# The sums of the input's quarters by accumulating transfers within SBUF, with the prompt's pieces spread over two stages

## The chip, the cores and the metric

The kernel runs on one core of one Trainium2 chip. The metric is the time of one execution on the device in microseconds (us), less being better. The five engines of the core appear under the profile's names: PE (TensorE matmuls; PEld is its loading of weights), DVE (VectorE), ACT (ScalarE), POOL (GpSimd) and SP (SyncE, which here only issues transfers).

## What is computed

One layer of a hybrid network is applied to 1024 tokens of a sample and to 128 tokens of a prompt, in f32, with a model width of 1024. Cut to what matters:

```python
h = rmsnorm(x, norm_g) * (1 + scale) + shift              # scale, shift, gate from silu(cond) @ w_ada + b_ada
u, v, g_a, c_q, c_kv, k_rope, g_b = split(h @ w_in)       # widths 512, 512, 512, 256, 128, 64, 512
a_out = gelu(u) * mix128(rmsnorm(gelu(v))) * silu(g_a)    # mixing of positions in chunks of 128
q = rmsnorm(c_q) @ w_uq;  k, val = split(rmsnorm(c_kv) @ w_ukv)   # 4 heads, rotary part of 64
attn = softmax(q @ k.T / sqrt(192)) @ val                 # the sample also reads 256 cached context tokens
y = x + gate * (concat(a_out, attn * silu(g_b)) @ w_o)
out = rmsnorm(y, final_g)                                 # new c_kv and k_rope of the prompt are outputs too
```

The sample and the prompt use the same weights; the prompt reads only itself.

## The kernel before

Every operand of a matmul is kept as two numbers, a rounded **high** value and the **low** remainder, and a product is made of three matmuls: high by high, high by low, low by high. Whatever is prepared for PE therefore takes two elementwise operations: a cast to the high value (on ACT at line 543, or on POOL at line 117) and a subtraction that leaves the low one (on DVE at line 114 for weights and sums; line 968 for the prompt's weights).

The stages, by the time of the profile: loading, normalising and the projection of `v` (to about 75 us); the projection of `c_q`, `c_kv` and `k_rope` ("the latents' projection", accumulators `zacc`), the rest of `v`, the mixing of positions and the gate's vector (`gps`) to 153.5 us; the **product phases** (153.5 to 320.4 us); folds, rotary parts and transposes (to 353 us); attention (to 560 us); the output projection (to the end).

In the product phases the sample's tokens are multiplied by the weights of `u`, `g_a` and `g_b`: 12 blocks of 128 channels, taken in six pairs j. The tokens are cut in two halves and the features in two halves, so the input is four quarters A11, A12, A21, A22 (tiles `area..`, each 128 x 4 x 2 x 512: four k, and high and low). The 2 x 2 block product is made with seven products instead of eight. They are called phases 1, 2, 5, 6, 7, 4 and 3, in this order for the pairs, the last two alternating. Each (phase, pair) is 12 matmuls `pr` at line 828. Four phases read sums of the quarters in place of a quarter: S1 = A21 + A22 (phase 5), S2 = S1 - A11 (phase 6), S3 = A22 - S2 (phase 7), S4 = A12 - S2 (phase 3). `sum_steps` makes them for each k with nine additions of 128 x 512 (a quarter is the sum of its high and its low half, so adding a quarter takes two), lines 937 to 951, into tiles `ss` and `sta`/`stb`; 36 in all. `own` then splits a sum into high and low and writes it over a quarter that is no longer needed (`area10` in phases 5 and 7, `area00` in 6 and 3).

The weights of a (phase, pair) are loaded by SP into `wr` tiles (`raw_load`), combined where the phase needs a combination (`tsum`), and split into `wop0..` (high) and `wop1..` (low).

The prompt's 128 tokens are multiplied by the same weights apart: `prompt_steps`, 24 **pieces** (six pairs j, four y). A piece is a load into `praw` by SP, a cast into `pw0..`, a low half into `pw1..`, and six matmuls into the accumulator `pps` at line 977.

The order of the instructions on each engine is made ahead of the run by the class `Plan`, a list scheduler. A step has a key, engines that may do it, a cost in us for each, the steps that it depends on, a priority, and resources that it takes and gives back (buffer places: `slot`, `raw`, `praw`, `pw`, `st`). Among the steps that are ready the one with the smallest priority number goes first. `VG` steps go to DVE if it is free and to POOL otherwise. `lag` is the time after a step's cost until its result counts as there. The resulting rows are executed in order on each engine, which wait for one another by semaphores. The prompt's matmuls have the priorities `PROMPTP` (per pair), its loads `PROMPTL`; the first load waits for `openB`, the end of the mixing and the latents' projection.

Of the kernel before, what the change touches and what calls it, by code (L numbers as in the profile page):

```python
# [18 lines left out]
P = 128  # L19
# [10 lines left out]
PROMPTP = (7.2, 7.8, 8.6, 9.2, 9.8, 10.4)  # L30
PROMPTL = (1.605, 1.625, 1.645, 1.665, 1.685, 1.705)
# [11 lines left out]
class Plan:  # L43
# [8 lines left out]
    def run(self):  # L52
        left = sorted(self.steps, key=lambda s: s[:2])
        back = []
        now = 0.0
        while left:
            for b in [b for b in back if b[0] <= now]:
                back.remove(b)
                self.resources[b[1]] += 1
            moved = False  # L60
            for s in left:
                _, _, key, engs, cost, fn, deps, takes, gives, lag = s
                free = [n for n, e in enumerate(engs) if self.free[e] <= now + 1e-6]
                if not free or any(self.made.get(d, 1e9) > now + 1e-6 for d in deps):
                    continue
                if any(self.resources[r] < takes.count(r) for r in takes):
                    continue
                for r in takes:
                    self.resources[r] -= 1
                eng = engs[free[0]]  # L70
                if len(engs) > 1:
                    cost = cost[free[0]]
                    fn(self.engines[eng])
                else:
                    fn()
                self.free[eng] = now + cost
                self.made[key] = now + cost + lag
                self.made[key + "!"] = now + cost
                back += [(now + cost + lag, r) for r in gives]
                left.remove(s)  # L80
                self.log.append((now, cost, eng, key))
                moved = True
                break
            if not moved:
                later = [t for t in (*self.free.values(), *self.made.values(), *(b[0] for b in back)) if t > now + 1e-6]
                assert later, [(s[2], [d for d in s[6] if d not in self.made], s[7]) for s in left]
                now = min(later)
# [9 lines left out]
def tile_hymba_step(ctx: ExitStack, tc: tile.TileContext, I, O):  # L97
# [441 lines left out]
    VG, COST = "VG", (0.75, 1.3)  # L539
# [215 lines left out]
    order = {"load": None, "high": None, "prompt": ["openB"], "ph": []}  # L755
# [16 lines left out]
    def weight_steps(ph, j, prio):  # L772
# [8 lines left out]
        if ph in (5, 6, 4):  # L781

            def total(e):
# [3 lines left out]
                else:  # L787
                    e.tensor_tensor(tsum[j], r(0), tsum[j], op=ALU.subtract)
# [6 lines left out]
        elif ph == 7:  # L795

            def total(e):
                e.tensor_tensor(r(0), r(0), r(1), op=ALU.subtract)
                leave(keys[1])
# [15 lines left out]
        step(f"w{ph}{j}", "V", 0.75, low, [f"wh{ph}{j}"], prio, gives=gives)  # L815
# [39 lines left out]
    def result_steps(ph, j):  # L855
# [27 lines left out]
        elif ph == 6:  # L883
            def fn():
                uu[j] = place(j, 1, 0) if gb else pools["b1"].tile([P, 512], F32, tag=f"u{j}", name=f"uu{j}")
                V.tensor_tensor(uu[j], s1[j], bk(), op=ALU.add)
# [3 lines left out]
        elif ph == 7:  # L890
            step(f"c7{j}", "V", 0.75, lambda: V.tensor_tensor(zz[j], zz[j], bk(), op=ALU.add), [m, f"uz{j}"], 1)
# [4 lines left out]
        elif ph == 4:  # L896
            step(f"c4{j}", "V", 0.75, lambda: V.tensor_tensor(s1[j], s1[j], bk(), op=ALU.add), [m, f"c22s{j}"], 1, gives=("psa",))
# [13 lines left out]
    def sum_steps():  # L911

        for k in range(4):
            cell = {}

            def own(x, ph, deps, k=k):
                step(f"ah{ph}.{k}", SG, HIGH, lambda e: rounded(e, MOVING[ph][:, k, 0, :], x()), deps, 2.2 + PHP[ph])

                def low():
                    lo_of(MOVING[ph][:, k, 1, :], x(), MOVING[ph][:, k, 0, :])  # L920
                    if ph == 7:
                        leave(("st", "b", k))

                step(f"a{ph}.{k}", "V", 0.75, low, [f"ah{ph}.{k}"], 2.2 + PHP[ph], gives=("st", "slot") if ph == 7 else ())

            def st(name, k=k, cell=cell):
                cell[name] = place_for(("st", name, k), f"st{name}{k}", [512])
                return cell[name]

            def s_new(k=k):  # L930
                ss[k] = pools["b2"].tile([P, 512], F32, tag=f"ss{k}", name=f"ss{k}")
                return ss[k]

            q = lambda a, i, k=k: f32(a[:, k, i, :])

            def s1z(e, k=k, cell=cell):
                e.tensor_tensor(ss[k], ss[k], cell["a"], op=ALU.add)
                leave(("st", "a", k))

            step(f"s1x.{k}", VG, COST, lambda e, q=q, st=st: e.tensor_tensor(st("a"), q(A21, 0), q(A21, 1), op=ALU.add), ["openB"], 3.0 + 0.01 * k, takes=("st", "slot"))  # L940
            step(f"s1y.{k}", VG, COST, lambda e, q=q, s_new=s_new: e.tensor_tensor(s_new(), q(A22, 0), q(A22, 1), op=ALU.add), ["openB"], 3.0 + 0.01 * k)
            step(f"s1z.{k}", VG, COST, s1z, [f"s1x.{k}", f"s1y.{k}"], 2.9, gives=("st", "slot"))
            own(lambda k=k: ss[k], 5, [f"s1z.{k}"])
            step(f"s2x.{k}", VG, COST, lambda e, k=k, q=q: e.tensor_tensor(ss[k], ss[k], q(A11, 0), op=ALU.subtract), [f"a5.{k}"], 3.2 + 0.01 * k)
            step(f"s2y.{k}", VG, COST, lambda e, k=k, q=q: e.tensor_tensor(ss[k], ss[k], q(A11, 1), op=ALU.subtract), [f"s2x.{k}"], 3.1)
            own(lambda k=k: ss[k], 6, [f"s2y.{k}", f"m1{NJ - 1}.{k}"])
            step(f"s3x.{k}", VG, COST, lambda e, q=q, st=st: e.tensor_tensor(st("b"), q(A22, 0), q(A22, 1), op=ALU.add), [f"s2y.{k}"], 3.4 + 0.01 * k, takes=("st", "slot"))
            step(f"s3y.{k}", VG, COST, lambda e, k=k, cell=cell: e.tensor_tensor(cell["b"], cell["b"], ss[k], op=ALU.subtract), [f"s3x.{k}"], 3.3)
            own(lambda cell=cell: cell["b"], 7, [f"s3y.{k}", f"m5{NJ - 1}.{k}"])
            step(f"s4x.{k}", VG, COST, lambda e, k=k, q=q: e.tensor_tensor(ss[k], q(A12, 0), ss[k], op=ALU.subtract), [f"a6.{k}", f"s3y.{k}"], 3.6 + 0.01 * k)  # L950
            step(f"s4y.{k}", VG, COST, lambda e, k=k, q=q: e.tensor_tensor(ss[k], ss[k], q(A12, 1), op=ALU.add), [f"s4x.{k}"], 3.5)
            own(lambda k=k: ss[k], 3, [f"s4y.{k}", f"m6{NJ - 1}.{k}"])
# [5 lines left out]
    def prompt_steps(n, j, prio):  # L958
# [21 lines left out]
        for y in range(4):  # L980
# [4 lines left out]
            step(f"pw{j}{y}", VG, COST, lambda e, y=y: low(e, y), [f"ph{j}{y}"], 1.5, gives=("praw", "slot"))  # L985
# [23 lines left out]
        step(f"pa{j}", "S", 0.45, act, [f"pm{j}3", *deps], 1.5, takes=("slot",), gives=("pst",))  # L1009
        step(f"pt{j}", "T", 0.22, tr, [f"pa{j}"], 3, takes=("pst",), gives=("slot",))  # L1010
# [339 lines left out]
    with tc.manual_schedule(engines=engines):  # L1350
        plan.resources.update(psa=1, pst=2, slot=6, gv=3, ga=1, raw=4, wop=3, tmp=2, praw=2, pw=2, st=3, r2=1)
# [38 lines left out]
        for h in range(4):  # L1390
            qn_steps(0, 512, h, 19.5 + 0.1 * h, [f"s4y.{k}" for k in range(4)])
# [584 lines left out]
```

## Time and profile before

| | |
|---|---|
| median of 3 runs | 663.19 us (lowest 660.75) |
| profiled execution | 662.15 us, its span on the core 660.4 us |
| granted TensorE clock, mean | 0.973 |
| PE busy | 618.8 us, 94% |
| DVE busy | 437.3 us, 66% |
| ACT busy | 301.6 us, 46% |
| POOL busy | 225.4 us, 34% |
| moved by transfers | 60.48 MB, 92 GB/s over the span |
| chain that ended last | PE 75%, DVE 11%, issue 4%, DMA 4%, ACT 2%, POOL 2% |

The span is the time from the first to the last instruction on the core; the execution takes 1.75 us more. Busy time counts neither register and branch instructions nor the issuing of transfers. A stretch A:B is in us from the span's start. In a group's row, "128x512" is partitions by elements, "xN" the number of instructions, then busy time in us and the mean of one in ns, then the engine's idle time before them and what ended it.

### The profile page before, as it was taken

Reading aid. Unit: us, or ns where it says so; the run is one execution under the profiler, and the core shown is the slowest. Engines: PE = TensorE matmul, PEld = TensorE weight load, DVE = VectorE, ACT = ScalarE, POOL = GpSimd, SP = SyncE. Lnnn points to the kernel's source line nnn. Section 1 sums busy time; section 2 is a strip of 40 time slices with the busy share of each in tenths; the row PEclk is TensorE's granted clock in tenths of the full one; section 3 lists DMA queues with packets and bytes.
Section 4 is the critical chain, followed back from the end, with each engine's and each line's share of the span. In section 5 each row is a group of like instructions: output and inputs, shape, how many; then the busy total and the mean of one; then the engine's idle time right before and its main releaser. Section 6 shows DMA issues by size and latency. Waiting matters only on the chain.

```text
span 660.4 us, 9804 instructions
## 1 busy us (share of the span) xinstructions
PE 618.8 (94%) x3567; PEld 524.7 (79%) x3567; DVE 437.3 (66%) x874; ACT 301.6 (46%) x672; POOL 225.4 (34%) x203
## 2 busy tenths in 40 slices
PE   7799999999888899799988999999999999999995
PEld 6477887788667678578867799999999998888884
DVE  4334645525999978988476765667767766296755
ACT  4355873324333253355564655555555462132222
POOL 3523311106876667644452322223313332000001
PEclk9699999999878999999997999999999999999998
DMA  8971314302425562430010000000000012523221
GB/s 325 341 260 47 134 46 166 126 33 68 139 78 187 171 213 80 140 128 1 26 48 1 1 1 0 1 1 1 1 33 33 33 65 97 191 97 128 80 80 64
DMA packets 29840, 60.48 MB, mean 92 GB/s; under 512 B 3024, under 2 KB 13664, under 8 KB 29792
## 3 DMA queue, kind: packets, MB, share of 16 engines
q1 hardware_dynamic: 29648, 59.67, 26.6%
q8 instruction: 28, 0.46, 0.3%
q14 instruction: 20, 0.16, 0.1%
q10 hardware_dynamic: 144, 0.20, 0.1%
HBM read 55.03 MB, written 4.83 MB: 91 GB/s over the span
## 4 chain that ended last, share of the span: by engine, by line
PE 75%; DVE 11%; issue 4%; DMA 4%; ACT 2%; POOL 2%; SPq 0%; ACTq 0%; POOLq 0%; DVEq 0%
PE pr L828 11%; PE pT L1504 5%; PE w L1754 5%; PE w L1753 5%; PE w L1755 5%; PE s L1461 3%; PE o L1528 3%; PE o L1530 3%; PE s L1465 3%; PE s L1462 3%; PE s L1463 3%; PE o L1529 3%; PE s L1464 3%; PE vacc L390 3%; PE pps L977 2%
## 5 line engine op out<-in xcount | busy, mean ns | idle before, releaser
L828 PE MATMUL pr<-area,wop 128*128 128x512 f32 x504 | 128.4, 403 | 4.3 <-ACT wop L543 2.3
L828 PEld LDWEIGHTS pr<-area,wop 128*128 128x128 f32 x504 | 93.8, 193 | 25.5 <-ACT wop L543 3.6
L1452 POOL TENSOR_SCALAR e<-e,rs 128x1280 f32<-128x1280 f32 x32 | 43.0, 1344 | 141.2 <-DVE rs L1451 126.3
L114 DVE TENSOR_TENSOR pl<-pT,ph 128x512 fp32r<-128x512 f32 x81 | 55.4, 687 | 45.9 <-ACT ph L1508 45.7
L1446 ACT ACTIVATE e<-s,nb,scl 128x256 f32<-128x256 f32 x64 | 56.1, 881 | 39.3 <-DVE nb L1440 39.2
L1508 ACT CAST ph<-pT 128x512 fp32r<-128x512 f32 x80 | 45.5, 590 | 40.0 <-PE pT L1504 37.2
L1753 PE MATMUL w<-area,areap 128*128 128x512 f32 (+1 forms) x152 | 57.8, 381 | 0.0
L1755 PE MATMUL w<-area,ml 128*128 128x512 f32 (+1 forms) x152 | 57.5, 378 | 0.0
L1754 PE MATMUL w<-area,areap 128*128 128x512 f32 (+1 forms) x152 | 57.5, 378 | 0.0
L1504 PE MATMUL pT<-ident,e 128*128 128x128 f32 x320 | 47.9, 272 | 0.6 <-DVE pl L114 0.6
L1528 PE MATMUL o<-ph,vh 128*128 128x256 f32 x160 | 48.0, 300 | 0.0
L1530 PE MATMUL o<-ph,vl 128*128 128x256 f32 x160 | 45.0, 281 | 0.0
L1529 PE MATMUL o<-pl,vh 128*128 128x256 f32 x160 | 44.9, 280 | 0.0
L1504 PEld LDWEIGHTS pT<-ident,e 128*128 128x128 f32 x320 | 37.8, 140 | 4.3 <-DVE pl L114 1.5
L1436 DVE TENSOR_REDUCE m<-s 128x1 f32<-128x1024 f32 x32 | 38.9, 1216 | 2.5 <-PE s L1465 2.5
L1461 PE MATMUL s<-kch,area 128*128 128x512 f32 (+1 forms) x96 | 38.8, 404 | 0.8 <-DVE areap L114 0.8
L977 PE MATMUL pps<-pw,areap 128*128 128x256 f32 x144 | 25.9, 312 | 13.1 <-DVE pw L968 13.1
L977 PEld LDWEIGHTS pps<-pw,areap 128*128 128x128 f32 x144 | 23.6, 210 | 17.1 <-DVE pw L968 14.5
L1844 POOL TENSOR_TENSOR z<-y,fg 128x256 f32<-128x256 f32 (+1 forms) x3 | 3.0, 998 | 95.4 <-DVE y L1839 95.4
L1463 PE MATMUL s<-kch,area 128*128 128x512 f32 (+1 forms) x96 | 34.7, 361 | 0.0
L1462 PE MATMUL s<-kcl,area 128*128 128x512 f32 (+1 forms) x96 | 34.7, 361 | 0.0
L1465 PE MATMUL s<-krl,area 128*128 128x512 f32 (+1 forms) x96 | 34.7, 361 | 0.0
(377 smaller groups left out, 1560.4 us busy)
## 6 DMA issues: line engine op xcount, KB each, us to landing
wr<-in_w_t SPq DMA_DIRECT2D x54, 256.0 KB, 3.4
ada<-in_ada_ss SPq DMA_DIRECT2D x16, 512.0 KB, 6.7
praw<-in_w_t SPq DMA_DIRECT2D x24, 256.0 KB, 3.3
xr<-in_x SPq DMA_DIRECT2D x9, 512.0 KB, 3.8
adag<-in_ada_g SPq DMA_DIRECT2D x8, 512.0 KB, 3.7
wor<-in_w_o SPq DMA_DIRECT2D x8, 512.0 KB, 3.7
out_y<-y SPq DMA_DIRECT2D x8, 512.0 KB, 2.8
x<-in_x SPq DMA_DIRECT2D x6, 512.0 KB, 6.6
```

The source lines that it names most:

```text
L114: V.tensor_tensor(lo, src, f32(hi), op=ALU.subtract)
L828: T.matmul(ps, w[a][:, k, :], x[:, k, b, :], start=first and ph in FIRST, stop=last, skip_group_check=ph not in FIRST)
L977: T.matmul(out, areap[:, 2 * y + k, b, :], pw[y][a][:, :, k, :], start=y == 0 and k == 0 and i == 0, stop=y == 3 and k == 1 and i == 2)
L1446: S.activation(e[:, sl], src, AF.Exp, bias=nb, scale=scl[:, t : t + 1], accum_out=su[:, i : i + 1])
L1461: T.matmul(ps, qh_, kch[:, sl], start=True, stop=False)
L1504: T.transpose(ps[:, w : w + P], es[t, h][:, c * P : (c + 1) * P], ident)
L1528: T.matmul(o, vh[:, kt, :], ph[:, sl], start=c == 0, stop=False)
L1529: T.matmul(o, vh[:, kt, :], pl[:, sl], start=False, stop=False)
L1530: T.matmul(o, vl[:, kt, :], ph[:, sl], start=False, stop=c == n - 1)
L1753: T.matmul(ps, a, woh[k][:, c0:c1], start=k == 0, stop=False)
L1754: T.matmul(ps, a, wol[k][:, c0:c1], start=False, stop=False)
L1755: T.matmul(ps, b, woh[k][:, c0:c1], start=False, stop=k == NK - 1)
```

## The change

**Sums.** The four k are taken in two halves g of two k each, tiles `ss0` and `ss1` of 128 x 2 x 512. S1 starts as a copy of A21's low half by a transfer of SP within SBUF; three transfers issued by POOL then add A21's high, A22's low and A22's high half to it (`accum_op=ALU.add`, line 934 of the changed kernel). ACT negates the tile (scale -1), and two accumulating transfers add A11, which gives A11 - S1 = -S2. A copy of it and two transfers more give S3 = A22 - S2; two more in place give S4 = A12 - S2. In all 20 accumulating transfers (16 of 512 KB, 4 of 256 KB), five copies by SP and two negations stand in place of the 36 additions. Each accumulating transfer of a chain waits for the landing of the one before it. Since S2 is now negative, some signs turn in the weights' totals and in the results (`add` to `subtract`).

**Planner.** A step that two engines may do goes to the one on which it would end first. While DVE and POOL both work (`v` and `G`), the planner lengthens both steps. The costs of the accumulating transfers on POOL are an issue `ADDC` of 1.0 and a lag `ADDL` of 3.0.

**Prompt.** Three of the six pairs have lower priority numbers, for loads and matmuls alike; the loads may start after the last load of the latents' weights (`wq7`) in place of `openB`. `slot` goes from 6 to 5 with a place `po` of its own for the prompt's results, `raw` from 4 to 6, `st` from 3 to 2.

```diff
-PROMPTP = (7.2, 7.8, 8.6, 9.2, 9.8, 10.4)
-PROMPTL = (1.605, 1.625, 1.645, 1.665, 1.685, 1.705)
+PROMPTP = (3.5, 3.6, 3.7, 8.8, 9.6, 10.4)
+PROMPTL = (0.9, 0.91, 0.92, 1.645, 1.665, 1.685)
...
-                free = [n for n, e in enumerate(engs) if self.free[e] <= now + 1e-6]
-                if not free or any(self.made.get(d, 1e9) > now + 1e-6 for d in deps):
+                when = [(max(self.free[e.upper()], now) + (cost[n] if len(engs) > 1 else cost), n) for n, e in enumerate(engs)]
+                eng = engs[min(when)[1]]
+                if self.free[eng.upper()] > now + 1e-6 or any(self.made.get(d, 1e9) > now + 1e-6 for d in deps):
...
+                other = {"v": "G", "G": "V"}.get(eng)
+                if other and now < self.shares[other] - 1e-6:
+                    r = min(self.shares[other] - now, 2 * cost)
+                    mine, theirs = (0.5 * r, 0.3 * r) if eng == "v" else (0.3 * r, 0.5 * r)
+                    cost += mine
+                    self.free[other] += theirs
+                    self.shares[other] += theirs
...
-    VG, COST = "VG", (0.75, 1.3)
+    VG, COST = "vG", (0.72, 1.25)
+    ADDC, ADDL, LOWL = 1.0, 3.0, 0.5
...
-    order = {"load": None, "high": None, "prompt": ["openB"], "ph": []}
+    order = {"load": None, "high": None, "prompt": [f"wq{NK - 1}"], "ph": []}
...
-                V.tensor_tensor(uu[j], s1[j], bk(), op=ALU.add)
+                V.tensor_tensor(uu[j], s1[j], bk(), op=ALU.subtract)
...
+        def copy_step(key, g, dst, src, deps, prio):
+            step(key, "D", 0.85, lambda: nc.sync.dma_start(dst(), src()), deps, prio, lag=2.6)
+
+        def add_step(key, dst, src, deps, prio):
+            step(key, "g", ADDC, lambda: nc.gpsimd.dma_start(dst(), src(), accum_op=ALU.add), deps, prio, lag=ADDL)
...
+            step(f"s1a{g}", "D", 0.85, first, ["openB"], 1.2, lag=2.6)
+            add_step(f"s1b{g}", z, lambda g=g: q(A21, g, 0), [f"s1a{g}"], 1)
+            add_step(f"s1c{g}", z, lambda g=g: q(A22, g, 1), [f"s1b{g}"], 1)
+            add_step(f"s1d{g}", z, lambda g=g: q(A22, g, 0), [f"s1c{g}"], 1)
...
+            step(f"sn{g}", "S", 1.05, minus, [f"a5.{k}" for k in two], 3)
+            add_step(f"s2a{g}", z, lambda g=g: q(A11, g, 1), [f"sn{g}"], 1)
+            add_step(f"s2b{g}", z, lambda g=g: q(A11, g, 0), [f"s2a{g}"], 1)
...
+            add_step(f"s4a{g}", z, lambda g=g: q(A12, g, 1), [f"s3a{g}", *(f"a6.{k}" for k in two)], 1.5)
+            add_step(f"s4b{g}", z, lambda g=g: q(A12, g, 0), [f"s4a{g}"], 1.5)
...
-        plan.resources.update(psa=1, pst=2, slot=6, gv=3, ga=1, raw=4, wop=3, tmp=2, praw=2, pw=2, st=3, r2=1)
+        plan.resources.update(psa=1, pst=2, slot=5, po=1, gv=3, ga=1, raw=6, wop=3, tmp=2, praw=2, pw=2, st=2, r2=1)
```

What the change makes of the order is seen best on POOL, at the beginning of the product phases (weights of phases 1 and 2). A row is the line, the operation, the tile that it writes, an arrow and the tiles that it reads. `ss` are the sums, `sta` and `stb` their partners, `area10` is A21 (which S1 overwrites), `area00` A11 (S2), `area11` A22, `wop0PJ` the cast weights of phase P and pair J. Before:

```order
L941 TENSOR_TENSOR ss0_1567<-area11_115 128x512
L941 TENSOR_TENSOR ss1_1583<-area11_115 128x512
L117 TENSOR_SCALAR area10_114<-ss0_1567 128x512
L941 TENSOR_TENSOR ss2_1608<-area11_115 128x512
L940 TENSOR_TENSOR sta3_1624<-area10_114 128x512
L117 TENSOR_SCALAR wop014_1641<-wr1400_1132 128x512
L941 TENSOR_TENSOR ss3_1650<-area11_115 128x512
L117 TENSOR_SCALAR wop015_1663<-wr1500_1140 128x512
L944 TENSOR_TENSOR ss0_1567<-ss0_1567,area00_112 128x512
L945 TENSOR_TENSOR ss0_1567<-ss0_1567,area00_112 128x512
L947 TENSOR_TENSOR stb0_1711<-area11_115 128x512
```

The same place on POOL in the changed kernel, from the second accumulating transfer of each half on:

```order
L934 DMA ss0_1642<-area11_115 128x2x512
L934 DMA ss1_1654<-area11_115 128x2x512
L129 TENSOR_SCALAR wop014_1779<-wr1400_1121 128x512
L934 DMA ss0_1642<-area11_115 128x2x512
L934 DMA ss1_1654<-area11_115 128x2x512
L129 TENSOR_SCALAR wop015_1831<-wr1500_1190 128x512
L129 TENSOR_SCALAR area10_114<-ss0_1642 128x512
L129 TENSOR_SCALAR area10_114<-ss1_1654 128x512 x2
L129 TENSOR_SCALAR wop021_1890<-wr2110_1624 128x512
```

The additions have gone from POOL, and the casts of weights now stand between accumulating transfers, each of which waits on POOL for the landing of the one before it. Further on in the same rows stand the two transfers of S2's halves and, behind them, the last cast of phase 2:

```order
L934 DMA ss0_1642<-area00_112 128x2x512
L934 DMA ss1_1654<-area00_112 128x2x512
L799 TENSOR_TENSOR tsum1_1997<-wr5101_1964,wr5100_1936 128x512
L129 TENSOR_SCALAR area00_112<-ss0_1642 128x512 x2
L129 TENSOR_SCALAR wop025_2044<-wr2510_1860 128x512
```

On DVE, at the end of phase 1's weights, before (`pw1JY` is the low half of the prompt's piece of pair J and step Y):

```order
L937 TENSOR_TENSOR ss2_1608<-ss2_1608,sta2_1591 128x512
L114 TENSOR_TENSOR area10_114<-ss0_1567,area10_114 128x512
L114 TENSOR_TENSOR wop114_1642<-wr1400_1132,wop014_1641 128x512
L937 TENSOR_TENSOR ss3_1650<-ss3_1650,sta3_1624 128x512
L114 TENSOR_TENSOR wop115_1664<-wr1500_1140,wop015_1663 128x512
L968 TENSOR_TENSOR pw102_1674<-praw02_1632,pw002_1673 128x512
L968 TENSOR_TENSOR pw103_1687<-praw03_1645,pw003_1686 128x512
L114 TENSOR_TENSOR area10_114<-ss1_1583,area10_114 128x512
```

And the same place on DVE in the changed kernel:

```order
L126 TENSOR_TENSOR wop115_1832<-wr1500_1190,wop015_1831 128x512
L126 TENSOR_TENSOR area10_114<-ss0_1642,area10_114 128x512
L1010 TENSOR_TENSOR pw131_1851<-praw31_1812,pw031_1850 128x512
L126 TENSOR_TENSOR wop120_1867<-wr2010_1611,wop020_1866 128x512
L126 TENSOR_TENSOR area10_114<-ss0_1642,area10_114 128x512
L126 TENSOR_TENSOR area10_114<-ss1_1654,area10_114 128x512
```

The additions of line 937 are gone here as well, and the prompt's pieces that stand between are those of pair 3, no longer those of pair 0. Those of pair 0 now stand on PE among the matmuls of the latents' projection (`zacc`, token group 4) and the mixing (`mixp`), ahead of the product phases:

```order
L712 MATMUL zacc4_1317<-wqh6_1022,area11_115 128x448
L1019 MATMUL pps0_1128<-pw003_1283,areap_116 128x256 x2
L1019 MATMUL pps0_1128<-pw103_1284,areap_116 128x256
L1019 MATMUL pps0_1128<-pw003_1283,areap_116 128x256 x2
L1019 MATMUL pps0_1128<-pw103_1284,areap_116 128x256
L618 MATMUL mixp8_1431<-wsT_695,gv8_1266 128x128 x4
L710 MATMUL zacc4_1317<-wqh7_1037,area11_115 128x448
```

Before the first `pr` matmul stand six of the 24 pieces now, four of pair 0 and two of pair 1; before the change none did. Over the whole program PE executes the same number of matmuls.

More of the change, by code (lines that the diff above doesn't have):

```diff
@@ L55, in run @@
         now = 0.0
+        self.shares = {"V": 0.0, "G": 0.0}
         while left:
@@ L814, in weight_steps @@
         step(f"wh{ph}{j}", SG, HIGH, high, loaded + before, prio, takes=("wop", "slot", "slot"))
-        step(f"w{ph}{j}", "V", 0.75, low, [f"wh{ph}{j}"], prio, gives=gives)
+        step(f"w{ph}{j}", "v", 0.72, low, [f"wh{ph}{j}"], prio, gives=gives, lag=LOWL)
     CHAIN = {1: 1, 2: 1, 5: 5, 6: 6, 7: 6, 4: 6, 3: 3}
@@ L911, in sum_steps @@
     def sum_steps():
[L913 to L952, printed above, removed]
```

70 lines of the change are left out of this document (59 added, 11 removed).

## The prediction

> **What bounds the kernel now.** I read the page first, then the stretches of time, then the waits, then the chain, then single groups.
>
> ```profile
> PE 618.8 (94%) x3567; PEld 524.7 (79%) x3567; DVE 437.3 (66%) x874; ACT 301.6 (46%) x672; POOL 225.4 (34%) x203
> ```
>
> PE is busy for 94% of the span, so time can only come from where it isn't. The stretches show where (us, busy time per engine with the number of instructions, granted clock, DMA share, GB/s):
>
> ```profile
> core 0: us, PE busy (x) PEld busy (x) DVE busy (x) ACT busy (x) POOL busy (x), PEclk, DMA share, GB/s
> 153.50:246.70 93.20, 80.09 (x390) 67.16 (x389) 82.79 (x100) 37.43 (x73) 66.36 (x50) 0.93 0.46 150
> 246.70:291.40 44.70, 40.42 (x171) 30.94 (x170) 41.06 (x45) 16.90 (x29) 31.05 (x22) 1.00 0.38 121
> 291.40:320.40 29.00, 28.99 (x146) 24.09 (x147) 21.74 (x33) 15.42 (x27) 11.32 (x10) 1.00 0.11 32
> 320.40:353.20 32.80, 27.62 (x176) 23.32 (x174) 22.17 (x37) 21.62 (x43) 17.51 (x23) 0.98 0.08 25
> 100.00:153.50 53.50, 50.77 (x295) 43.03 (x295) 23.91 (x82) 16.00 (x60) 8.39 (x8) 1.00 0.28 94
> 180.00:200.00 20.00, 15.66 (x70) 13.02 (x68) 18.93 (x19) 8.22 (x14) 15.81 (x12) 0.83 0.29 95
> 220.00:240.00 20.00, 19.22 (x100) 15.93 (x99) 15.32 (x22) 8.35 (x15) 11.86 (x10) 1.00 0.64 211
> ```
>
> The first row is the stretch of product phases 1, 2 and 5, with all of the prompt's pieces. PE stands still for 93.20 - 80.09 = 13.1 us there, and the granted clock is 0.93. DVE is busy for 82.79 of 93.20 us, POOL for 66.36. The waits of that stretch name the cause, and the chain shows one case:
>
> ```profile
> PE pps L977 <- DVE pw L968: 13.1, 6, 3.3
> ...
> 162.36 0.71 PE pps L977 x6
> 163.08 0.71 PE pr L828 x3
> ...
> 184.40 1.75 DVE pw L968
> 186.20 1.22 PE pps L977 x4
> 187.42 1.28 PE pr L828 x3
> ```
>
> All 13.1 us are PE waiting for `pw`, the low half of a piece of the prompt's weights, which DVE makes late. After such a wait three `pr` matmuls take 1.28 us, before any wait 0.71: the clock drops behind the long waits (0.83 in 180 to 200). That costs another 0.07 x 93.2 = 6.5 us. This stretch is bound by **DVE and POOL**, the later ones mostly by PE.
>
> Why DVE is late is seen in the means of its groups in the stretch, and of POOL's:
>
> ```profile
> L968 DVE TENSOR_TENSOR pw<-praw,pw 128x512 fp32r<-128x512 f32 x19 | 18.9, 1010 | 1.4 <-ACT pw L543 0.8 <-POOL pw L117 0.5
> L951 DVE TENSOR_TENSOR ss<-ss,area 128x512 f32<-128x512 f32 x2 | 3.6, 1782 | 0.0
> L948 DVE TENSOR_TENSOR stb<-stb,ss 128x512 f32<-128x512 f32 x3 | 2.0, 679 | 0.0
> L945 POOL TENSOR_TENSOR ss<-ss,area 128x512 f32<-128x512 f32 x3 | 5.1, 1685 | 0.1
> L117 POOL TENSOR_SCALAR wop<-wr 128x512 fp32r<-128x512 f32 x5 | 4.8, 957 | 0.6 <-DVE pw L968 0.6
> ...
> L117 POOL TENSOR_SCALAR area<-wor 128x512 fp32r<-128x512 f32 x16 | 10.1, 642 | 7.2 <-DMA wor<-in_w_o 7.2
> L940 POOL TENSOR_TENSOR sta<-area 128x512 f32<-128x512 f32 x1 | 1.3, 1297 | 1.0 <-PE pr L828 1.0
> ...
> 190.00:192.00 2.00, 2.00 (x6) 1.55 (x6) 1.45 (x3) 1.59 (x4) 1.01 (x1) 0.57 0.00 0
> 195.00:203.00 8.00, 5.35 (x28) 4.55 (x28) 8.00 (x6) 3.21 (x5) 7.30 (x5) 0.94 0.52 165
> ```
>
> The same 128x512 addition takes DVE 0.68 us at its best (L948; two of the three lie in 190 to 192 us, where POOL is at 1.01 of 2.00) and 1.78 us in 195 to 203 us (L951, POOL at 7.30 of 8.00). POOL is stretched too: its casts from 0.64 to 0.96 us, its additions from 1.30 to 1.69.
>
> **The change, part by part.** *Sums.* 36 additions go, 16 on DVE and 20 on POOL. What the planner puts in their place is in the order: in the stretch DVE goes from 74 wide rows to 60 (it takes over some of POOL's other work), POOL from 52 wide rows to 23, of which two-input ones 35 to 7. At the pw mean of 1.01 us the 14 rows are 14 us of DVE; if POOL's part in the contention went entirely, the other 60 would fall to 0.68 us, 20 us more. DVE's 82.8 us become 49 to 69. The stretch without its losses is 93.2 - 19.6 = 73.6 us, with those added below about 77, so DVE would be busy for 63% to 89% of it. Slice 220 to 240 has DVE at 77%, and there PE loses 0.78 of 20 us at clock 1.00. I take that rate: 0.039 x 77 = **3.0 us of waits remain**, without a drop of the clock. The ends are 0 and 13.1.
>
> *The additions as transfers.* POOL now issues 20 of them, 16 of 512 KB and 4 of 256 KB; SP issues 5 copies. No row shows a transfer within SBUF, one that accumulates, or one issued by POOL. The nearest:
>
> ```profile
> xr<-in_x SPq DMA_DIRECT2D x9, 512.0 KB, 3.8
> wvr<-in_w_v SPq DMA_DIRECT2D x8, 256.0 KB, 9.8
> ...
> L1784 SPq DMA_DIRECT2D xr<-in_x x9: 328/383/430, 556.9 to 626.3; - x9
> ...
> 0.00:20.00 20.00, 14.73 (x92) 12.36 (x92) 10.98 (x41) 7.78 (x14) 5.20 (x9) 1.00 0.91 340
> ...
> 291.41 15.93 PE pr L828 x69
> ...
> L417 ACT ACTIVATE x<-x,x3r 128x1024 f32<-128x1024 f32 x2 | 2.3, 1148 | 6.6 <-DVE x3r L134 6.6
> ```
>
> A step of a chain is an issue (0.4 us), a landing (3.8 us) and the other half's 0.5 MB on the same queues (0.5 MB at 340 GB/s is 1.5 us): an estimate of **5.7 us** from these rows. The ends are 3.8, and 9.8 + 0.4 = 10.2.
>
> The sums themselves are needed late: S1 not before phase 5, about 41 us after the first product, and its three steps with the copy end near 21. What is exposed is POOL. It waits in order at each chained transfer, and the hi casts `wop` of the next products stand behind. The last of phase 2, `wop025`, stands behind five steps in series (three of S1, two of S2) and about 11 us of single work: the copy 3.8 and the other half's issue 0.4, two casts of S1 1.3 (0.64 each, unstretched), its low 0.7, the negation on ACT 1.1, a `tsum` 1.3 (by L940), two casts of S2 1.3, its own cast and low 1.3. PE needs it after 11 products (12 matmuls at 15.93 / 69 = 0.231 us, 2.77 each) and 11 pieces (0.71 each), 38.3 us. The point is (38.3 - 11.2) / 5 = **5.4 us per step**; each us above it costs up to 5. At 5.7 that is 1.5 us; the first step is issued with both halves' queues empty, so I take **1.0 us**. The ends: 0, and 24 at 10.2.
>
> The Trainium skill ("DMA: Bandwidth & Descriptors", "Anatomy of one DMA") fits a POOL-issued transfer as 2.0 us plus bytes / 436 GB/s, an estimate of 3.2 us for 512 KB; by it this term is 0 and the sum 646.6. No row of this trace shows one.
>
> *Prompt's pieces.* Of 24 pieces six (36 matmuls, 6 x 0.71 = 4.3 us of PE) now stand among the latents' projection, before the first product; none did. PE does them either way, so the work costs 0. In 100 to 153.5 DVE is at 23.9 of 53.5 us and ACT at 16.0, which hides casts and lows. Their loads stand in SP's queue between those of the gate's weights, and behind them wait SP's later loads. PE could lose there what it loses now per piece, 13.1 / 24 = 0.55 us, for six 3.3; or fill its present 53.5 - 50.8 = 2.7 us of gaps. I take **+1.0**.
>
> *At nothing:* two negations on ACT (1.15 us each; ACT is at 37 of 93 us), turned signs (same instructions), the copies' issue on SP (0.4 us each), the prompt's own place `po`. Stretch 246.7 to 291.4 keeps its 4.3 us. The sums' own work there, by the windows view cut to the tile `ss` (columns now DVE, ACT, POOL, clock, DMA):
>
> ```profile
> 246.70:291.40 44.70, 6.28 (x4) 1.88 (x3) 2.94 (x3) 1.00 0.38 121
> ```
>
> It is 6.28 us of DVE and 2.94 of POOL, in 41.06 and 31.05. Without ACT's idle time the negations would cost 2.3.
>
> **The sum**, against the profiled execution of 662.15 us (span 660.4 and 1.75 around it; the runs' median is 663.19): 662.15 - 13.1 - 6.5 + 3.0 + 1.0 + 1.0 = **647.6 us**. By the median's 2% (13.3 us, about what a measurement tells from no change) the borders are 649.9 and 676.5.
>
> **Rivals.** *Transfers too slow, slower than before.* The queues are shared: the share in the stretch is 0.46 now. A full queue moves 340 / 0.91 = 374 GB/s, so 0.54 x 374 = 202 GB/s are free. A step of both halves is 1.05 MB, 5.2 us if each byte counts once, which fits; 10.4 us if an accumulating transfer counts twice, since it also fetches its destination. Then POOL's casts are 5 x (10.4 - 5.4) = 25 us late, in place of my 1.0: 671.6. Equal to before at 8.5 us per step. For it speaks the landing of 9.8 us at share 0.91; against it, that the loads of weights can give way, and the 3.8. The Trainium skill ("Collectives: The Full Stack", "The bandwidth ceiling") states that a reduction in the transfer needs two source reads and runs at half the rate of a copy; by that rule this is the case that comes, and 671.6 the time. The trace has nothing that accumulates.
>
> *The change doesn't relieve DVE.* The planner gives DVE work that POOL had, and POOL still casts beside it (casts stretch DVE too). At 89% busy the waits are nearer half of now, 6.5, with half the clock's loss, 3.3: 662.15 - 6.5 - 3.3 + 1 + 1 = 654.4. For it: 19 pw rows on DVE before, 17 in the stretch after. Against: POOL's two-input work falls to a fifth.
>
> *All of it goes well.* No residual waits, no stall, the 2.7 us of gaps filled: 662.15 - 19.6 - 2.7 = 639.9.
>
> **How the numbers follow.** Forecast 0.46 (641 to 654, two thirds of it below 649.9: 0.32); all well 0.12 (635 to 641); DVE not relieved 0.20 (652 to 660, within 2%); slow transfers 0.22 (658 to 690; 0.10 above 676.5). So faster 0.32 + 0.12 = 0.44, slower 0.10, the same 0.46. The range 638 to 668 leaves out half of the all-well case (0.06) and about 0.12 of the slow one.
>
> **What would show it.** Right: in the first stretch PE's waits for pw near 3 us, the granted clock 1.00 there, DVE's wide operations near 0.7 to 0.8 us, and steps of the chains of 4 to 6 us between POOL's issues. Wrong: PE waiting for `wop` cast by POOL, with POOL waiting for a transfer ahead of it; DVE at over 85% with pw late; PE gaps among the latents' projection.

## The result: slower by 0.8%, and the profile after

| | before | after |
|---|---|---|
| median | 663.19 us (660.75 to 663.97, 5 runs) | **668.08 us** (666.92 to 669.28, 6 runs) |
| ratio of the means | | 1.0083, 95% interval 1.0059 to 1.0107 |
| span of the profiled execution | 660.4 us | 665.8 us |

A sixth run of the kernel before took 1005.53 us, a slow state, and is left out. The forecast was 647.6 us, the range 638 to 668; the measured time lies just above it. The change makes the kernel slower by 0.6% to 1.1%, less than the 2% that the prediction calls the same.

The stretches of the changed kernel follow, cut at the same places of the program as before: the first product begins at 157.15 us, and the matmuls `pr` that had been issued by 246.7 and 291.4 us now are by about 255.0 and 296.6. The columns are PE, PE's loading, DVE, ACT, POOL, the granted clock, the DMA share and GB/s:

```profile
100.00:157.10 57.10, 55.79 (x335) 47.76 (x335) 24.42 (x84) 19.87 (x72) 9.18 (x10) 1.00 0.36 121
157.10:255.00 97.90, 79.86 (x347) 63.51 (x347) 50.15 (x85) 34.24 (x66) 45.99 (x44) 0.84 0.99 242
255.00:296.60 41.60, 38.91 (x170) 31.47 (x169) 37.84 (x43) 15.04 (x25) 28.34 (x21) 1.00 0.41 132
```

The second row holds the loss. The stretch takes 97.9 us where it took 93.2, although six pieces (4.3 us of PE) have left it. DVE is at 50.15 of 97.9 us, where it was at 82.79 of 93.2: the relief came. Yet PE stands still for 18.0 us (13.1 before), and the clock is 0.84 (0.93 before), by the prediction's way of reckoning another 0.16 x 97.9 = 16 us. The DMA share is 0.99: no queue time is left. The waits between 153 and 293 us (waiting line, the line waited for: us, times, longest) say for what the engines wait:

```profile
POOL ss L934 <- DMA ss<-area: 28.9, 8, 7.1
...
ACT pw L556 <- DMA praw<-in_w_t: 21.0, 7, 6.1
DVE wop L126 <- POOL wop L129: 11.7, 5, 5.3
ACT area L556 <- DMA ss<-area: 11.1, 2, 5.9
...
PE pps L1019 <- DVE pw L1010: 5.4, 4, 3.7
...
PE pr L842 <- POOL wop L129: 3.6, 1, 3.6
PE pr L842 <- DVE wop L126: 3.4, 1, 3.4
...
PE poT L1038 <- ACT po L1033: 2.9, 1, 2.9
...
PE pps L1019 <- ACT pw L556: 2.6, 2, 2.0
```

POOL waits 28.9 us for transfers to land, DVE behind it for POOL's casts, and PE behind both. The last row is of another kind: the prompt's casts on ACT wait 21.0 us for their own loads, which land late in the full queues (a median of 4.9 us, 3.3 before), and PE waits 2.6 us for these casts. The start of the chains on POOL (start, duration; in brackets the wait before it):

```profile
158.97 1.37 POOL L934 DMA_DIRECT2D ss<-area  x1 [1.06 <-DMA ss<-area]
161.52 1.20 POOL L934 DMA_DIRECT2D ss<-area  x1 [1.17 <-DVE zzt L145]
162.28 1.10 POOL L129 TENSOR_SCALAR wop<-wr 128x512 fp32r<-128x512 f32 x1
166.34 1.20 POOL L934 DMA_DIRECT2D ss<-area  x1 [2.96 <-DMA ss<-area]
170.54 1.20 POOL L934 DMA_DIRECT2D ss<-area  x1 [3.00 <-DMA ss<-area]
171.31 1.10 POOL L129 TENSOR_SCALAR wop<-wr 128x512 fp32r<-128x512 f32 x1
176.07 1.22 POOL L934 DMA_DIRECT2D ss<-area  x1 [3.67 <-DMA ss<-area]
...
205.03 1.05 POOL L129 TENSOR_SCALAR wop<-wr 128x512 fp32r<-128x512 f32 x1
...
228.69 1.19 POOL L934 DMA_DIRECT2D ss<-area  x1 [7.11 <-DMA ss<-area]
229.44 1.74 POOL L802 TENSOR_TENSOR tsum<-wr,tsum 128x512 f32<-128x512 f32 x1
236.31 1.20 POOL L934 DMA_DIRECT2D ss<-area  x1 [5.13 <-DMA ss<-area]
237.09 1.72 POOL L802 TENSOR_TENSOR tsum<-wr,tsum 128x512 f32<-128x512 f32 x1
```

The first half's steps begin at 158.97, 166.34 and 176.07 us: 7.4 and 9.7 us apart, where the prediction took 5.7 for a step. One cast stands between two of them, and the next one waits. The cast at 205.03 is `wop025`, the one that the prediction watched. A second hole stands at 228 to 237 us, where the totals of phase 6 (`tsum`) wait behind S4's transfers. The queues (packets, MB, share of 16 engines' span), and the landing time of the 512 KB steps, a median of 8.3 us:

```profile
q1 hardware_dynamic: 30624, 61.76, 27.4%
q0 software_dynamic: 4928, 9.44, 8.0%
...
ss<-area POOLq DMA_DIRECT2D x14, 512.0 KB, 8.3
```

8.0% of 665.8 us are 53 us for 9.44 MB, or 177 GB/s; the other queue moved 61.76 MB in 27.4%, 338 GB/s.

### The profile page after: what moved, and what is told of

The parts are those of the page before. It is cut to its first block, busy times and chain, and to the rows that moved or that the text cites. A ratio compares the mean times of both kernels' runs of the same rounds, so it can differ in the third digit from the quotient of the medians.

```text
span 665.8 us, 9825 instructions
## 1 busy us (share of the span) xinstructions
PE 621.6 (93%) x3567; PEld 527.4 (79%) x3567; DVE 405.2 (61%) x874; ACT 299.8 (45%) x669; POOL 194.2 (29%) x192
## 3 DMA queue, kind: packets, MB, share of 16 engines
q1 hardware_dynamic: 30624, 61.76, 27.4%
q0 software_dynamic: 4928, 9.44, 8.0%
## 4 chain that ended last, share of the span: by engine, by line
PE 71%; DMA 8%; DVE 8%; issue 6%; POOL 4%; ACT 3%; SPq 0%; POOLq 0%; ACTq 0%; DVEq 0%
PE pr L842 8%; PE pT L1546 5%; PE w L1797 5%; PE w L1795 5%; PE w L1796 5%; DMA ss<-area 4%; PE s L1503 3%; PE o L1570 3%; PE o L1572 3%; PE s L1504 3%; PE s L1507 3%; PE s L1505 3%; PE o L1571 3%; PE s L1506 3%; PE vacc L402 3%
## 5 line engine op out<-in xcount | busy, mean ns | idle before, releaser
L842 PE MATMUL pr<-area,wop 128*128 128x512 f32 x504 | 131.3, 413 | 9.9 <-POOL wop L129 3.6
L842 PEld LDWEIGHTS pr<-area,wop 128*128 128x128 f32 x504 | 97.0, 199 | 33.1 <-DVE wop L126 5.6
L1506 PE MATMUL s<-krh,area 128*128 128x512 f32 (+1 forms) x96 | 34.6, 361 | 0.0
L1797 PEld LDWEIGHTS w<-area,ml 128*128 128x128 f32 x152 | 28.6, 188 | 5.4
L1795 PEld LDWEIGHTS w<-area,areap 128*128 128x128 f32 x152 | 28.6, 188 | 4.9
```

What stands on the lines that cost most here:

```text
L842: T.matmul(ps, w[a][:, k, :], x[:, k, b, :], start=first and ph in FIRST, stop=last, skip_group_check=ph not in FIRST)
L1795: T.matmul(ps, a, woh[k][:, c0:c1], start=k == 0, stop=False)
L1797: T.matmul(ps, b, woh[k][:, c0:c1], start=False, stop=k == NK - 1)
```

## The experiments

The theory at first, theory 1: an accumulated byte costs the queues twice a copied one. Its rival, theory 2: the way over POOL is slow whatever is moved. Ratios are to runs of the kernel before beside them.

**1. Transfers alone.** A kernel of its own.

```diff
+    for _ in range(6):
+        G.dma_start(z0, s0, accum_op=ALU.add)      # A; B with a second chain z1, C to E without accum_op
```

> A kernel with nothing but transfers of 512 KB within SBUF; the computation is left out. Six stages: A one chain of six that accumulate, B two such chains alternating, C one chain of plain copies issued by POOL, D two of these, E one chain of plain copies issued by SP, F stage B again beside 24 loads of 256 KB of weights. In the changed kernel an accumulating transfer took 8.3 us from issue to landing (median of 14), with two chains and loads under way. Theory 1 (the queues are full, an accumulated byte costs them twice a copied one): A about 4 to 5 us per step, C 3 us or less, B about twice A per pair and D about half of B, F slower than B, with the queues' share near 1 in B and F. Theory 2 (the way over POOL is slow, whatever is moved): A and C alike at 7 to 8 us, E at 4 us, B no longer per step than A, share well below 1.

POOL's issues in stage A, B, C and F, each issue waiting for the landing of the one before it in its chain:

```profile
9.35 0.87 POOL L54 DMA_DIRECT2D z<-s  x1 [3.95 <-DMA z<-s]
14.12 0.86 POOL L54 DMA_DIRECT2D z<-s  x1 [3.90 <-DMA z<-s]
...
45.22 0.86 POOL L59 DMA_DIRECT2D z<-s  x1 [2.00 <-DMA z<-s]
48.07 0.86 POOL L58 DMA_DIRECT2D z<-s  x1 [1.99 <-DMA z<-s]
50.89 0.86 POOL L59 DMA_DIRECT2D z<-s  x1 [1.96 <-DMA z<-s]
...
75.97 0.54 POOL L63 DMA_DIRECT2D z<-s  x1 [2.59 <-DMA z<-s]
79.09 0.53 POOL L63 DMA_DIRECT2D z<-s  x1 [2.58 <-DMA z<-s]
...
159.52 0.86 POOL L77 DMA_DIRECT2D z<-s  x1 [4.18 <-DMA z<-s]
163.91 0.86 POOL L76 DMA_DIRECT2D z<-s  x1 [3.53 <-DMA z<-s]
168.31 0.86 POOL L77 DMA_DIRECT2D z<-s  x1 [3.54 <-DMA z<-s]
```

One chain alone takes 4.8 us per step, two take 5.7, a chain of copies 3.1, and two chains beside loads of weights 8.8 in the lines shown. The windows of stage A, B and D (POOL's busy time in the middle; share and GB/s at the end):

```profile
9.35:33.00 23.65, 0.00 (x0) 4.31 (x5) 1.00 0.58 111
45.00:65.00 20.00, 0.00 (x0) 6.07 (x8) 1.00 1.00 189
...
96.00:110.00 14.00, 0.00 (x0) 4.77 (x9) 1.00 0.81 327
```

Two accumulating chains fill the queues at 189 GB/s; copies reach 327 at a share of 0.81, an estimated 404 at a full one. Theory 1 stands, with one miss: a second chain beside the first makes a step 5.7 us long, not twice 4.8, since one chain alone takes only 0.58 of the queues. Theory 2 falls: a chain of copies over POOL takes 3.1 us per step, and SP's copies in stage E land in 2.9.

**2. Plain copies in the changed kernel.**

```diff
-            step(key, "g", ADDC, lambda: nc.gpsimd.dma_start(dst(), src(), accum_op=ALU.add), deps, prio, lag=ADDL)
+            step(key, "g", ADDC, lambda: nc.gpsimd.dma_start(dst(), src()), deps, prio, lag=ADDL)
```

> The changed kernel with plain copies in place of the 20 accumulating transfers, same sizes, same order, same waits; this leaves the additions of the sums out. Theory 1 (accumulating moves bytes at half the rate): the steps of the chains fall from 8.3 us to about 4, PE's losses behind wop and pw go, and the time is near the forecast's 648 to 655. Theory 2 (issuing through POOL and waiting there in order): the steps stay at 7 to 8 us and the time at 665 to 668.

648.5 us, ratio 0.9795 (0.9767 to 0.9823). Against 668.1 in the same order, accumulating costs **19.6 us**. The queue's row:

```profile
q0 software_dynamic: 2624, 9.44, 3.9%
...
ss<-area POOLq DMA_DIRECT2D x14, 512.0 KB, 5.5
```

The same 9.44 MB in 3.9% of 646.6 us, 25 us: half the time, in about half the packets. A copy lands in 5.5 us, not in the 4 expected, and the first half's steps begin at 161.10, 166.88 and 173.40 us, 5.8 and 6.5 us apart.

**3 and 4. The other two parts of the change.** Sums back on the engines, planner and prompt's place kept; and the prompt's part alone on the kernel before. In the latter's order the first pair's result of the prompt is multiplied into the mix before the mixing has written it, so a part of the prompt's output differs; the instructions are the same.

```diff
-            add_step(f"s1b{g}", z, lambda g=g: q(A21, g, 0), [f"s1a{g}"], 1)
+            step(f"s1x.{k}", VG, COST, lambda e, q=q, st=st: e.tensor_tensor(st("a"), q(A21, 0), q(A21, 1), op=ALU.add), ["openB"], 3.0 + 0.01 * k, takes=("st", "slot"))
...
```

> The changed kernel with the 36 additions back on DVE and POOL as before; planner (earliest finish, shares, costs) and the prompt's new place stay. If the transfers alone cost the time (both theories), this is faster than 668 and, since the prompt's six early pieces relieve DVE of up to 6 of 24 waits, faster than before: 13.1 x 6 / 24 = 3.3 us of waits and a quarter of the clock's 6.5, about 658. Rival: the new planner and the prompt's place make the order worse, and this is at 668 too or above.

```diff
-PROMPTP = (7.2, 7.8, 8.6, 9.2, 9.8, 10.4)
+PROMPTP = (3.5, 3.6, 3.7, 8.8, 9.6, 10.4)
-PROMPTL = (1.605, 1.625, 1.645, 1.665, 1.685, 1.705)
+PROMPTL = (0.9, 0.91, 0.92, 1.645, 1.665, 1.685)
-    order = {"load": None, "high": None, "prompt": ["openB"], "ph": []}
+    order = {"load": None, "high": None, "prompt": [f"wq{NK - 1}"], "ph": []}
...
```

> The kernel before with the prompt's part alone (priorities, loads after the latents' weights, a place of its own for the results). The prompt's part as forecast: PE's early pieces cost +1 in the latents' projection and save a quarter of the waits for pw (3.3 us) and of the clock's loss (1.6): about 659. Rival: the early loads and pieces only shift the waits, 663; or POOL and DVE are no less crowded and the time is 665 or more.

Number 3 took 648.9 us, 0.9795 (0.9764 to 0.9827): **this version, without a transfer in the sums, is about 2% faster than before**, more than expected. Number 4 took 670.6, 1.0131 (1.0105 to 1.0158), not the 659 expected but the rival's 665 or more: on the old planner PE now waits for weights that DVE makes late (waits from 150 to 300 us):

```profile
PE pr L828 <- DVE wop L114: 14.5, 7, 6.2
```

**5 and 6. POOL's row, or the queues?**

Casts of the product phases so dear on POOL that all go to ACT (5):

```diff
-    SG, HIGH = "SG", (0.62, 0.75)
+    SG, HIGH = "SG", (0.62, 30.0)
```

> The changed kernel with the casts of the product phases (weights, prompt's pieces, sums) all planned on ACT; POOL issues the transfers and makes totals, but no cast stands behind a transfer that waits. Theory 1 (what costs the 19 us over plain copies is POOL's order: casts blocked behind chained transfers): most of it comes back, 650 to 656. Theory 2 (the chains and loads themselves land late in full queues, whoever casts): 662 to 668, with PE then waiting for wop and pw from ACT, and ACT for loads and sums.

The planner told of a landing near the measured one (6):

```diff
-    ADDC, ADDL, LOWL = 1.0, 3.0, 0.5
+    ADDC, ADDL, LOWL = 1.0, 7.0, 0.5
```

> The changed kernel with the planner's lag of an accumulating transfer at 7.0 in place of 3.0, so that issue and lag are near the 8.3 us measured; the planner then puts other work of POOL between the transfers instead of behind them. Theory 1 (POOL's order): about 655, since casts now come ahead of the waits. Theory 2 (queues): 662 to 670; the sums are planned later and later phases wait for them.

Number 5: 672.9 us, 1.0152 (1.0129 to 1.0174); number 6: 654.0 us, 0.9876 (0.9839 to 0.9914). The first lies above both theories' ranges and contradicts the one that it is POOL's row as such; the second agrees with that one. The waits of number 5 show why (150 to 300 us):

```profile
ACT area L556 <- DMA ss<-area: 18.7, 4, 12.1
...
PE pps L1019 <- ACT pw L556: 12.5, 2, 10.4
```

The block has moved: ACT now waits at a sum's cast for its transfer, up to 12.1 us, and the prompt's casts behind it are late. So the reading, which number 9 tests, is that what counts is not the engine that waits but the planner: told of 1.0 + 3.0 us, it puts the waiting step ahead of others that are ready. With 7.0 the steps are as long (160.50, 167.74, 176.59 us) but two casts stand between them:

```profile
160.50 1.37 POOL L934 DMA_DIRECT2D ss<-area  x1 [1.35 <-DMA ss<-area]
163.20 1.20 POOL L934 DMA_DIRECT2D ss<-area  x1 [1.32 <-DMA ss<-area]
163.97 2.20 POOL L129 TENSOR_SCALAR wop<-wr 128x512 fp32r<-128x512 f32 x2
167.74 1.21 POOL L934 DMA_DIRECT2D ss<-area  x1 [1.57 <-DMA ss<-area]
171.99 1.20 POOL L934 DMA_DIRECT2D ss<-area  x1 [3.04 <-DMA ss<-area]
172.75 2.20 POOL L129 TENSOR_SCALAR wop<-wr 128x512 fp32r<-128x512 f32 x2
176.59 1.22 POOL L934 DMA_DIRECT2D ss<-area  x1 [1.64 <-DMA ss<-area]
```

**7 and 8. The planner alone; the change without the prompt's part.** The same edit, in number 3 and in the changed kernel:

```diff
-PROMPTP = (3.5, 3.6, 3.7, 8.8, 9.6, 10.4)
+PROMPTP = (7.2, 7.8, 8.6, 9.2, 9.8, 10.4)
-PROMPTL = (0.9, 0.91, 0.92, 1.645, 1.665, 1.685)
+PROMPTL = (1.605, 1.625, 1.645, 1.665, 1.685, 1.705)
-    order = {"load": None, "high": None, "prompt": [f"wq{NK - 1}"], "ph": []}
+    order = {"load": None, "high": None, "prompt": ["openB"], "ph": []}
```

> The planner's part alone: sums on DVE and POOL, the prompt's priorities and loads as before. With the prompt's part too it was 648.9, the prompt's part alone 670.6 on the old planner. Theory A (the planner's truer costs alone set the order right; the prompt's place is worth little): 649 to 653. Theory B (the gain needs both, as the pieces leave the crowded stretch): 657 to 663.

> The changed kernel with the prompt's priorities and loads as before; transfers and planner stay. All 24 pieces with their 6 MB of loads stand in the stretch of the transfers again. If the transfers' cost is the same 19 us whatever stands beside, this is the planner alone plus 19, some 670 to 680. Rival: what the loads take from the transfers counts, and six more pieces there cost more, above 680.

Number 7: **650.5 us, 0.9818 (0.9793 to 0.9842)**; number 8: 666.0, 1.0041 (1.0022 to 1.0060). Number 8 is below both of its ranges: more of the prompt's loads beside the transfers cost nothing. The gain is the planner's, taken with the lag of the low halves and the buffer places that came with it. The prompt's part makes 1.5 us less with the sums on engines and 2 more with transfers; the intervals overlap in both cases. With all additions still on DVE and POOL, number 7 has in 150 to 250 us, the kernel before first:

```profile
150.00:250.00 100.00, 86.89 (x422) 73.12 (x422) 86.97 (x103) 39.38 (x76) 71.39 (x55) 0.93 0.45 144
```

```profile
150.00:250.00 100.00, 92.88 (x462) 75.19 (x460) 95.27 (x91) 40.95 (x77) 76.26 (x54) 1.00 0.50 156
```

DVE is busier than ever, 95 of 100 us, and PE does more, at the full clock. Its waits there:

```profile
PE pps L991 <- DVE pw L982: 4.0, 8, 1.0
PE pr L842 <- DVE wop L126: 2.9, 6, 0.8
```

No longer six of up to 3.3 us, but fourteen of at most 1.0, 6.9 us in all.

**9 to 12. What accumulating costs once it is planned.** Number 9 has the edits of 5 and 6, number 10 those of 6 and 2, number 11 a lag of 10.0. Number 12 has lag 7 and only S3 and S4 by transfers; S1 and S2 are made by five additions for each k:

```diff
-            add_step(f"s1b{g}", z, lambda g=g: q(A21, g, 0), [f"s1a{g}"], 1)
...
+                step(f"s1x.{k}", VG, COST, lambda e, v=v, s_new=s_new, i=i: e.tensor_tensor(s_new()[:, i, :], v(A21, 0), v(A21, 1), op=ALU.add), ["openB"], 3.0 + 0.01 * k)
+                step(f"s1y.{k}", VG, COST, lambda e, v=v, x=x: e.tensor_tensor(x(), x(), v(A22, 0), op=ALU.add), [f"s1x.{k}"], 2.95)
...
```

> Lag 7 and all casts of the product phases on ACT: the two edits that gave 654.0 and 672.9 apart. Theory P (the loss is planned: whatever stands in an engine's row behind an instruction that waits for a transfer is late, on POOL as on ACT, and a lag near the real landing cures it): the 672.9 falls by as much as 668.1 did, 14 us or more, to 652 to 659. Theory Q (ACT's row simply can't hold the casts, or the full queues do it): it stays above 665.

> Lag 7 with plain copies in place of the accumulating transfers, which leaves the additions out. At lag 3 accumulating cost 668.1 - 648.5 = 19.6 us over copying. Theory P: in an order planned for slow landings the rate matters little, so this is at 648 to 652, at most 6 us under the 654.0 with accumulation. Theory Q (queues that are full cost as such): accumulating costs its 10 us or more here too, 644 or less.

> The changed kernel with the planner's lag of an accumulating transfer at 10.0. With the issue's 1.0 this is above every step of the chains seen (7 to 10 us). Theory P: the same as lag 7 or a little better, 650 to 655; what is planned late costs nothing until the sums are late for their phases. Rival: the sums come too late for phases 5 and 6, 657 or more.

> Lag 7, with S1 and S2 by 20 additions on DVE and POOL and only S3 and S4 by transfers (10 that accumulate, 3 copies). With all additions on the engines it was 648.9 and DVE was busy for 49.8 of 50 us in the middle of the product phases; with all of them as transfers and lag 7 it was 654.0 and the queues' share was 1.0. Halving both should leave PE fewer waits than either: 644 to 648. Rival: DVE's fullness costs PE little, the transfers' chains more, and it lies between, 649 to 654.

| | us | ratio, 95% interval |
|---|---|---|
| 9, casts on ACT | 656.1 | 0.9895 (0.9856 to 0.9934) |
| 10, plain copies | 643.3 | 0.9711 (0.9683 to 0.9738) |
| 11, lag 10 | 655.0 | 0.9895 (0.9855 to 0.9935) |
| 12, half by transfers | 649.4 | 0.9800 (0.9774 to 0.9825) |

Casts on ACT fall by 16.8 us with the lag (672.9 to 656.1), as theory P has it. But accumulating still costs 654.0 - 643.3 = 10.7 us over copying, more than the 6 that P allowed and about what Q did. Of the 19.6 us at lag 3, 8.9 went with the order; 10.7 are left to accumulating as such. Plain copies gain from lag 7 as well (648.5 to 643.3): their steps of 5.8 and 6.5 us were longer than the 4.0 planned, too. Lag 10 is no better than 7. Half by transfers is no better than none (648.9): the hoped-for 644 to 648 didn't come.

**13 to 15.** Out of number 7, the lengthening of steps (13):

```diff
-                if other and now < self.shares[other] - 1e-6:
+                if other and False:
```

> The planner alone (650.5 us, sums on the engines, the prompt as before) without the lengthening of steps while DVE and POOL both work. Theory R (the 12.4 us come from planning DVE's and POOL's stretched durations: rows of DVE no longer come later than planned, so PE's order and DVE's agree): 659 to 664. Theory S (they come from the choice of the engine that ends first, the lags or the changed costs): 649 to 653.

Out of number 7, the choice of the engine that ends first (14):

```diff
-                eng = engs[min(when)[1]]
+                free = [e for e in engs if self.free[e.upper()] <= now + 1e-6]
+                eng = free[0] if free else engs[0]
...
```

> The planner alone with the rule of before for the engine (DVE if it is free, else POOL), the lengthening kept. Theory R: 649 to 654, since the durations are still planned as they are. Theory S (the choice of the engine that ends first carries it): 658 to 664.

Number 15 has the edits of 6 and 8.

> Transfers at lag 7 with the prompt's priorities and loads as before. The prompt's part cost 2 us with transfers at lag 3 (666.0 against 668.1) and gained 1.5 us with the sums on engines. If its early loads keep the queues freer for the transfers, this is above 654.0, at 656 to 660; if they count for nothing there, 652 to 655.

653.4 (0.9866, 0.9841 to 0.9892), 652.2 (0.9846, 0.9815 to 0.9878) and 655.8 (0.9908, 0.9873 to 0.9943): neither the lengthening of steps nor the choice of engine carries the planner's 12.4 us (before against number 7), and the prompt's part counts for little at lag 7 too.

**16 to 18.** What was left. The low halves' lag alone, on the kernel before (16; the prompt's low halves alike):

```diff
-        step(f"w{ph}{j}", "V", 0.75, low, [f"wh{ph}{j}"], prio, gives=gives)
+        step(f"w{ph}{j}", "V", 0.75, low, [f"wh{ph}{j}"], prio, gives=gives, lag=0.5)
...
```

> The kernel before with one edit of the planner: the low halves of weights and of the prompt's pieces get a lag of 0.5 in place of 0.1 until PE may be planned to use them. Theory U (PE's six long waits came from matmuls planned just behind a low half that DVE finishes late; a little slack reorders them): 650 to 655. Otherwise: 660 to 664.

The places of buffers alone, on the kernel before (17):

```diff
-        plan.resources.update(psa=1, pst=2, slot=6, gv=3, ga=1, raw=4, wop=3, tmp=2, praw=2, pw=2, st=3, r2=1)
+        plan.resources.update(psa=1, pst=2, slot=5, po=1, gv=3, ga=1, raw=6, wop=3, tmp=2, praw=2, pw=2, st=3, r2=1)
...
```

> The kernel before with the change's buffer places alone: six raw loads of weights ahead in place of four, five shared places and one of its own for the prompt's results. Theory V (loads further ahead and the own place keep pieces from coming late): 650 to 655. Otherwise: 660 to 664.

And the lag out of number 7 (18):

```diff
-    ADDC, ADDL, LOWL = 1.0, 3.0, 0.5
+    ADDC, ADDL, LOWL = 1.0, 3.0, 0.1
```

> The planner alone (650.5) with the low halves' lag back at 0.1, all else kept. Theory U: 657 to 663. Theory V, or that several edits each help a little: 649 to 654.

664.3 (1.0019, 0.9996 to 1.0041), 662.9 (1.0007, 0.9991 to 1.0024) and 654.0 (0.9875, 0.9845 to 0.9904). Alone on the old planner neither helps. Of the three parts taken out of the new one, the lag costs 3.5 us, the lengthening 2.9 and the choice of engine 1.8, of which the last two are hardly clear of the intervals. Several edits make the gain together; which pair would do, and what the changed costs do by themselves, wasn't tried.

## Why the prediction was wrong

- **"A step of a chain is 5.7 us"** is the term that failed, and with it the +1.0 for POOL's stall. It put the price of a copy, and of a copy's bytes, on a transfer that accumulates. Two chains alone do take 5.7 us, but at a share of 1.00, and beside loads 8.8; in the kernel a step lands after 8.3. Plain copies in the same order (number 2) took 19.6 us less. The prediction's formula gives at 8.3 us 5 x (8.3 - 5.4) = 14.5 in place of 1.0, 661.1 in all; the rest is in the next points.
- **The place of the stall was right, and not the only one.** `wop025` was needed at 157.15 + 38.3 = 195.5 us; its cast began at 205.03, and PE waited 3.6 us for it, of 18.0 in all. The hole at 228 to 237 us, totals of phase 6 behind S4's transfers, was not in the prediction. Nor was ACT, whose casts of sums wait 11.1 us for landings, or the prompt's loads, for which its casts wait 21.0.
- **"Transfers too slow"**, at 0.22, was the case that came: half the rate by the row of queue 0, the threshold of 8.5 us per step nearly met, 668.1 against its 671.6. The nearness of the two times is luck: the 671.6 has all of its loss at `wop025`, 19.6 us of relief, and nothing for the planner. The Trainium skill ("Collectives: The Full Stack", "The bandwidth ceiling") says, of collectives, that a reducing transfer reads two sources and runs at half a copy's rate; stages B and D, 189 against an estimated 404 GB/s, agree.
- **"-13.1 and -6.5, DVE relieved"**: DVE's side came as forecast (82.8 to 50.2 us, at the low end of 49 to 69; the low halves `pw` from 1010 to 777 ns). But "this stretch is bound by DVE and POOL" was wrong. Number 7 halves the waits and loses no clock there, with DVE at 95%. What PE lost it lost to the order of the rows; which of the planner's assumptions set it wrong is not shown. Without additions and with lag 7 (number 10) the relief brings 648.9 - 643.3 = 5.6 us more, not 19.6; at lag 3 (number 2) it brings 0.4.
- **The planner's terms were missing.** The prediction costed at nothing that the planner chooses by earliest finish and with other costs; it is the larger gain of the change, 12.4 us. That number 2, with copies, comes within 1 us of the forecast's 647.6 is luck for this reason: the planner's gain stands there in place of the relief's.
- **Prompt's pieces, +1.0**: the first product begins 3.7 us later (157.15 against 153.47) with 4.3 us more of PE work ahead of it, -0.6. That is within its bounds.

The change's balance by the runs: planner and prompt's place about -14 us (ratio 0.9795, number 3); from there the transfers add 19.1. Of these 14.1 went with lag 7 (668.1 to 654.0), and the 5.1 left are 10.7 for accumulating less 5.6 for DVE's relief.

## What to carry to other kernels

A transfer that accumulates took the queues twice as long as a copy of the same bytes here (8.0% against 3.9% of the span): count its bytes twice when you set it against free queue time, and give a planner the lag measured beside the kernel's loads, 8.3 us, not that of one alone, 4.8 per step. Where rows are fixed ahead of time, an instruction that waits for a transfer holds up what stands behind it, so a lag that is too short costs more here than one that is too long (3 against 7: 14 us; 7 against 10: 1, within the intervals). And an engine at 90% beside a waiting one isn't yet the bound: first see whether what is waited for could have stood earlier in its row.

## What the runs showed of the hardware

Accumulating in f32 within SBUF about halved the rate at which full queues moved bytes, 189 GB/s against 404 (estimated from 327 at a share of 0.81), and took 4928 packets where the copies of the same bytes took 2624. A copy issued by POOL took 3.1 us per step for 512 KB; the Trainium skill ("DMA: Bandwidth & Descriptors", "Anatomy of one DMA") gives an estimate of 3.2, and the accumulating one took 4.8. The granted clock did not follow the sum of PE's waits alone. In 150 to 250 us it was 1.00 in number 14 with 9.7 us of waits, none over 1.5, and 1.00 in number 7 with 6.9, none over 1.0; it was 0.93 in number 12 with only 7.9 us, of which two waits alone make 4.0 and 3.3. Numbers 14 and 12:

```profile
150.00:250.00 100.00, 90.29 (x447) 73.12 (x446) 96.10 (x84) 44.23 (x84) 82.58 (x56) 1.00 0.47 150
```

```profile
150.00:250.00 100.00, 92.18 (x445) 77.62 (x442) 75.69 (x109) 38.30 (x76) 51.05 (x44) 0.93 0.70 193
```

So a few long waits went with a lower clock than more time in short ones. A long wait doesn't always do it: number 11 had one of 4.0 us among 8.9, and its clock was 0.99. These are comparisons of kernels, not an experiment on the clock.
